# The last MLP's second pair of down chunks: eight of 16 k tiles in seven products instead of four, in three of its four quarters

## The chip, the cores and the metric

The kernel runs on one core of a Trainium2 chip. Its engines work side by side, each through its own instructions in order: PE (matrix multiply; the profile lists its weight loads apart as PEld), DVE (vector), ACT (scalar), POOL, and SP, which only issues transfers here. The metric is the device time of one execution in microseconds (us). A matrix product writes to PSUM; all other operands lie in SBUF, and weights come from HBM by DMA.

## The reference

A trunk of two layers on 256 tokens of width 2048. Each layer has a token mixer, an attention to a memory of 256 rows and an MLP with hidden width 8192; at the end stands a final norm. All in float32. The change touches the MLP of the second layer only:

```python
def squared_relu_mlp(h, w_up, w_down):
    return jnp.square(jax.nn.relu(h @ w_up)) @ w_down

for i in range(DEPTH):                      # 2 layers
    ...
    x = x + squared_relu_mlp(rms_norm(x, g_ff[i]), f_w_up[i], f_w_down[i])
return rms_norm(x, g_final)
```

## The kernel before

**Precision.** A float32 operand is split into a rounded high part and a remainder: ACT casts the high part (`whi`, `hh`), DVE subtracts to get the low part (`wlo`, `hl`), both in `split` (lines 103 and 104). A product is three matmuls, high by high, low by high and high by low. Every weight chunk of 128 x 1024 that is multiplied therefore costs ACT one cast and DVE one subtraction, whatever PE does with it.

**Tiling of the MLP.** `mlp` goes through the hidden width in four quarters `b`. Each quarter has an up part, which makes 2048 hidden features (four pairs of `hh` and `hl` tiles, eight calls of `gemm_feat`, four weight chunks each), and a down part, which multiplies these 16 k tiles by the quarter's rows of `w_down` and adds the result to `x`. The down part has four chunks `n` of 512 output columns. In the last MLP (`nxt.closing`) they go in two pairs, (0, 1) and (2, 3), through `gemm_seven`; only in the last quarter the chunks 2 and 3 go by plain products.

**Seven products.** For two halves of the tokens, two chunks of columns and two halves of some k tiles, a product has eight blocks of six matmuls. `gemm_seven` makes it of seven blocks, with sums of the hidden values (`token_sums`, made once per quarter) and four sums of weights. Named by the halves (k half, column chunk) of the weights, these sums are T1 = raw(0,1) - raw(0,0), T2 = raw(1,1) - T1, T3 = raw(1,1) - raw(0,1) and T4 = raw(1,0) - T2; each is one DVE subtraction of 128 x 1024, and each is then split like a chunk. The first four k tiles go this way in every pair (tiles `ws` and `run`; four of their split results go to a pair of buffers of their own, `own`). With `ahead`, four further k tiles go the same way (tile `more`: four raw chunks, and two slots for sums). What is left goes in plain products, `direct`, one weight chunk for two blocks. So a pair with `ahead` has 14 blocks of seven products and 8 plain chunks, a pair without has 7 and 12. Before the change, the first pair of every quarter has `ahead`, and the second has not.

**What sets the order.** A scheduler orders each engine's instructions by their priority and by what is free, when the kernel is built; on the chip each engine keeps that order. SP's queue issues all weight loads in one order, and a load whose buffer is still read holds back all behind it. Buffers: four for `wraw` (plain chunks), four for `ws`, three for the split pair `whi`/`wlo`, two for `own`, one tile `more` at a time. `block_ahead` (line 726) loads the four raw chunks of `more` and returns a function that makes its first three sums (lines 733 to 735); the fourth is made in `gemm_seven` (line 827). `gather` (line 687) adds a finished block to `x`; `keep` (line 800) has ACT copy an intermediate sum from PSUM to `more`.

Of the kernel before, what the change touches and what calls it, by code (L numbers as in the profile page):

```python
# [13 lines left out]
ALU = mybir.AluOpType  # L14
# [3 lines left out]
D = 2048  # L18
S = 256
KT = D // P  # L20
NB = 512
NCH = D // NB
KB = 2
# [6 lines left out]
DFF = 4 * D  # L30
# [8 lines left out]
class Trunk:  # L39
# [604 lines left out]
    def mlp(self, x, layer, cur, nxt):  # L644
        nc, a, tc = self.nc, self.a, self.tc
        wu, wd = a["f_w_up"][layer], a["f_w_down"][layer]
        hT = cur.act
        with tc.tile_pool(name="ml", bufs=4, reuse_waits="tile") as mp:
            r2 = mp.tile([P, 32 if layer else 24], F32, name="r2", bufs=1)[:, 0:2]
            ws = lambda: mp.tile([P, KB * NB], F32, name="ws", bufs=4)  # L650
            run = lambda: mp.tile([P, KB * NB], F32, name="run", bufs=1)
            kept = lambda i: more[:, 6 + i // 2, i % 2 * NB:i % 2 * NB + NB]
            self.fifth = None if nxt.closing else mp
            for b in range(DFF // D):
                hid = []
                for n in range(NCH):
                    h = mp.tile([P, 4, S], F32R, name="hh")
                    l = mp.tile([P, 4, S], F32R, name="hl")
                    rs = []
                    for i in range(2):  # L660
                        r = mp.tile([P, 2, S], F32, name="r", bufs=2)
                        self.gemm_feat(hT, wu, 2 * (NCH * b + n) + i, r)
                        nc.vector.scalar_tensor_tensor(out=r, in0=r, scalar=0.0, in1=r, op0=ALU.max, op1=ALU.mult)
                        self.split(h[:, 2 * i:2 * i + 2], l[:, 2 * i:2 * i + 2], r)
                        rs.append(r)
                    hid.append((h, l))
                    if nxt.closing and n == 0:
                        sums = []
                    if nxt.closing and n < 2:
                        sums.append(self.token_sums(ws(), lambda: mp.tile([P, 4, 2, P], F32R, name="sums", bufs=4), *rs))  # L670
                    if nxt.closing and n == NCH - 2:
                        more = self.act.tile([P, 8, KB * NB], F32, name="more", tag="act")
                        ahead = self.block_ahead(more, wd, b * KT)
                if nxt.closing:
                    ahead[-1]()
                if nxt.closing:
                    own = lambda: mp.tile([P, KB * NB], F32R, name="own", bufs=2)
                    nxt.room = lambda: mp.tile([P, 2, NB], F32, name="g", tag="ws", bufs=4)
                if b == 0:
                    rstd = cur.rstd()  # L680
                    nc.vector.tensor_tensor(out=r2, in0=rstd, in1=rstd, op=ALU.mult)
                if b == DFF // D - 1 and not nxt.closing:
                    nxt.start()

                def gather(t, n, part, cs=None):
                    xc = x[:, t, cs or slice(n * NB, (n + 1) * NB)]
                    nc.vector.scalar_tensor_tensor(out=xc, in0=part, scalar=r2[:, t:t + 1], in1=xc,
                                                   op0=ALU.mult, op1=ALU.add)

                for n in range(NCH):  # L690
                    end = b == DFF // D - 1
                    if nxt.closing and not (end and n >= NCH - 2):
                        if n % 2 == 0:
                            self.gemm_seven((ws, run, kept), lambda kt, t: [f[:, kt % 4, t * P:(t + 1) * P]
                                                                            for f in hid[kt // 4]],
                                            sums, wd, n, b * KT, gather, own=own, ahead=ahead if n == 0 else None)
                            if end:
                                nxt.start()
                    elif nxt.closing and end and n == NCH - 1:
                        self.gemm_last(hid, wd, n, b * KT, lambda t, acc: nxt.finish(x, t, lambda cs: gather(  # L700
                            t, n, acc[:, cs.start - n * NB:cs.stop - n * NB], cs)))
                        break
                    else:
                        acc = self.gemm_hid(hid, wd, n, b * KT)
                        for t in range(2):
                            gather(t, n, acc[:, t, :])
                    if end:
                        self.at(4 + n if nxt.closing and n < 2 else 1, lambda n=n: nxt.chunk(x, n))

            self.fifth = None  # L710
# [12 lines left out]
        self.split(sh, sl, s)  # L723
        return sh, sl

    def block_ahead(self, tile, w, k0):
        v = self.nc.vector
        raw = {(i, j): tile[:, 2 * i + j] for i in range(2) for j in range(2)}
        for (i, j), t in raw.items():
            self.fed = self.nc.sync.dma_start(out=t.rearrange("p (k c) -> p k c", k=KB), in_=w[j, k0 // KB + 2 + i]).ins  # L730

        def add():
            v.tensor_tensor(out=tile[:, 4], in0=raw[0, 1], in1=raw[0, 0], op=ALU.subtract)
            v.tensor_tensor(out=tile[:, 5], in0=raw[1, 1], in1=tile[:, 4], op=ALU.subtract)
            v.tensor_tensor(out=raw[0, 1], in0=raw[1, 1], in1=raw[0, 1], op=ALU.subtract)
        return raw, tile[:, 4], tile[:, 5], add

    def gemm_seven(self, tiles, token, sums, w, n0, k0, gather, end=None, own=None, ahead=None):

# [3 lines left out]
        v = nc.vector  # L745
        kc0 = k0 // KB
        ws, run, kept = tiles
        raw, half = {}, lambda t: t.rearrange("p (k c) -> p k c", k=KB)
# [45 lines left out]
        def whole(*a):  # L794
            for _ in direct(*a):
                pass
# [16 lines left out]
        block((0, 0), 0, 1, raw[1, 0], far.get((1, 0)))  # L813
        whole(1, 1)
        v.tensor_tensor(out=run, in0=raw[1, 1], in1=run, op=ALU.subtract)
        summed((1, 0), 1, run, t2)
        gather(0, n0, m1)
        u2 = keep((1, 0), 2)
        whole(1, 1)
        v.tensor_tensor(out=raw[0, 1], in0=raw[1, 1], in1=raw[0, 1], op=ALU.subtract)  # L820
        summed((1, 0), 2, raw[0, 1], far.get((0, 1)))
        gather(0, n0 + 1, u2)
        u3 = keep((1, 0), 3)
# [4 lines left out]
        block((1, 0), 1, 1, run, t1)  # L828
        whole(1, 1)
        summed((0, 1), 3, raw[1, 1], far.get((1, 1)))  # L830
        v.tensor_tensor(out=u3, in0=u3, in1=m5, op=ALU.add)
        whole(0, 0)
        gather(1, n0 + 1, u3)
        while len(todo[0]) > 1 or len(todo[1]) > 1:
            j = len(todo[1]) > len(todo[0])
            whole(j, j)
        ends = [direct(0, 1), direct(1, 0)]
        for keys in (((1, 0), (0, 1)), ((0, 0), (1, 1))):
            for e in ends:
# [774 lines left out]
```

## Time and profile before

| what | value |
|---|---|
| median of 3 runs | 2776.56 us (2775.83 to 2779.21) |
| the profiled execution | 2781.7 us, its span 2780.0 us, granted TensorE clock 0.998 |
| PE busy in the span | 2755.7 us (99%), 14996 matmuls |
| DVE, ACT busy | 2025.2 us (73%), 1410.3 us (51%) |
| DMA | 593.74 MB, 214 GB/s on average |
| last MLP's quarter 0: up part | from about 2076 to 2167.4 us |
| its first pair, second pair | 2167.4 to 2208.5, 2208.5 to 2250.9 us |
| quarters 1, 2 and 3: first pair starts at | 2340.0, 2512.5 and 2685.0 us |

Times in rows of the profile are from the start of the span. The duration of a matmul in a row includes its way through the array; matmuls overlap, so that the distance between two starts, and not the duration, is what one costs.

### The profile page before, as it was taken

Reading aid. Unit: us, or ns where it says so; the run is one execution under the profiler, and the core shown is the slowest. Engines: PE = TensorE matmul, PEld = TensorE weight load, DVE = VectorE, ACT = ScalarE, POOL = GpSimd, SP = SyncE. Lnnn points to the kernel's source line nnn. Section 1 sums busy time; section 2 is a strip of 40 time slices with the busy share of each in tenths; the row PEclk is TensorE's granted clock in tenths of the full one; section 3 lists DMA queues with packets and bytes.
Section 4 is the critical chain, followed back from the end, with each engine's and each line's share of the span. In section 5 each row is a group of like instructions: output and inputs, shape, how many; then the busy total and the mean of one; then the engine's idle time right before and its main releaser. Section 6 shows DMA issues by size and latency. Waiting matters only on the chain. (4 is left out here: it accounts for less than half of the span.)

```text
span 2780.0 us, 39477 instructions
## 1 busy us (share of the span) xinstructions
PE 2755.7 (99%) x14996; PEld 2330.6 (84%) x14996; DVE 2025.2 (73%) x2788; ACT 1410.3 (51%) x1805; POOL 187.0 (7%) x331
## 2 busy tenths in 40 slices
PE   9999999999999999999999999999999999999998
PEld 7888888888888888888887888888888888888887
DVE  6765756778888878787567657557777868778685
ACT  6445544555534444444556445445555545446454
POOL 0100000001011111120212100000000000000000
PEclk9999999999999999999999999999999999999999
DMA  8766665547788888886879766565557466564655
GB/s 295 225 201 232 200 182 181 169 159 237 216 278 260 261 257 259 265 259 214 237 246 272 221 200 228 176 194 154 182 175 226 148 215 199 194 220 148 217 182 158
DMA packets 194174, 593.74 MB, mean 214 GB/s; under 512 B 44096, under 2 KB 45168, under 8 KB 193472
## 3 DMA queue, kind: packets, MB, share of 16 engines
q1 hardware_dynamic: 153456, 537.46, 61.2%
q0 software_dynamic: 40000, 52.71, 6.8%
q8 instruction: 117, 1.92, 0.3%
q10 hardware_dynamic: 528, 1.06, 0.1%
q14 instruction: 73, 0.60, 0.1%
HBM read 567.51 MB, written 23.46 MB: 213 GB/s over the span
## 5 line engine op out<-in xcount | busy, mean ns | idle before, releaser
L104 DVE TENSOR_TENSOR wlo<-wraw,whi 128x1024 fp32r<-128x1024 f32 (+1 forms) x877 | 1065.1, 1221 | 442.2 <-ACT whi L103 435.9
L103 ACT CAST whi<-wraw 128x1024 fp32r<-128x1024 f32 (+1 forms) x877 | 920.6, 1051 | 833.2 <-PE acc L764 180.3
L174 PE MATMUL acc<-act,whi 128*128 128x512 f32 x3072 | 742.0, 392 | 3.3 <-ACT whi L103 2.2
L174 PEld LDWEIGHTS acc<-act,whi 128*128 128x128 f32 x3072 | 563.2, 188 | 114.0 <-ACT whi L103 2.6
L179 PEld LDWEIGHTS acc<-act,wlo 128*128 128x128 f32 x3072 | 396.3, 192 | 17.8 <-DVE wlo L104 2.1
L179 PE MATMUL acc<-act,wlo 128*128 128x256 f32 x3072 | 404.6, 284 | 1.5 <-DVE wlo L104 1.0
L159 PE MATMUL acc<-whi,act 128*128 128x512 f32 x1472 | 369.5, 393 | 5.6 <-ACT whi L103 5.6
L159 PEld LDWEIGHTS acc<-whi,act 128*128 128x128 f32 x1472 | 274.8, 189 | 62.8 <-ACT whi L103 5.8
L764 PE MATMUL acc<-whi,act 128*128 128x512 f32 x864 | 232.9, 392 | 0.1
L855 PE MATMUL acc<-whi,hl 128*128 128x512 f32 x544 | 212.7, 391 | 0.0
L854 PE MATMUL acc<-whi,hh 128*128 128x512 f32 x544 | 212.6, 391 | 0.0
L159 PE MATMUL acc<-wlo,act 128*128 128x512 f32 x736 | 197.6, 390 | 0.2 <-DVE wlo L104 0.2
L764 PEld LDWEIGHTS acc<-whi,act 128*128 128x128 f32 x864 | 160.4, 188 | 36.7 <-ACT ends L800 1.9
L159 PEld LDWEIGHTS acc<-wlo,act 128*128 128x128 f32 x736 | 138.3, 188 | 29.8 <-DVE wlo L104 1.0
L857 PE MATMUL acc<-wlo,hh 128*128 128x512 f32 x544 | 145.8, 389 | 0.0
L764 PE MATMUL acc<-wlo,act 128*128 128x512 f32 x432 | 133.1, 390 | 0.0
L764 PE MATMUL acc<-whi,hh 128*128 128x512 f32 x338 | 132.7, 393 | 0.0
L764 PE MATMUL acc<-whi,hl 128*128 128x512 f32 x338 | 131.6, 389 | 0.0
L190 ACT COPY r<-acc 128x512 f32<-128x512 f32 x64 | 37.7, 589 | 165.9 <-PE acc L174 165.8
L855 PEld LDWEIGHTS acc<-whi,hl 128*128 128x128 f32 x544 | 102.1, 188 | 22.2 <-issue 1.0
L854 PEld LDWEIGHTS acc<-whi,hh 128*128 128x128 f32 x544 | 102.1, 188 | 21.4 <-issue 0.2
L857 PEld LDWEIGHTS acc<-wlo,hh 128*128 128x128 f32 x544 | 102.1, 188 | 21.4 <-issue 0.2
(375 smaller groups left out, 2813.3 us busy)
## 6 DMA issues: line engine op xcount, KB each, us to landing
wraw<-in_f_w_up SPq DMA_DIRECT2D x256, 512.0 KB, 4.6
wraw<-in_f_w_down SPq DMA_DIRECT2D x212, 512.0 KB, 5.1
wraw<-in_x_w_q SPq DMA_DIRECT2D x64, 512.0 KB, 4.2
wraw<-in_x_w_k SPq DMA_DIRECT2D x64, 512.0 KB, 4.2
wraw<-in_b_w_out SPq DMA_DIRECT2D x64, 512.0 KB, 4.4
wraw<-in_a_w_in SPq DMA_DIRECT2D x63, 512.0 KB, 4.7
wraw<-in_x_w_v SPq DMA_DIRECT2D x48, 512.0 KB, 4.3
wraw<-in_x_w_o SPq DMA_DIRECT2D x48, 512.0 KB, 4.2
```

The source lines that it names most:

```text
L103: self.nc.scalar.copy(out=hi, in_=src)
L104: return self.nc.vector.tensor_tensor(out=lo, in0=src, in1=hi.bitcast(F32), op=ALU.subtract).ins
L159: nc.tensor.matmul(out[t], a[:, kt, sl], b[:, kk, :], start=st and a is ah, stop=en)
L174: nc.tensor.matmul(acc[:, f, :], hi[:, kk, sl], both[:, kt].rearrange("p a s -> p (a s)"), start=first and kk == 0, stop=last and kk == FK ...
L179: nc.tensor.matmul(acc[:, f, 0:S], lo[:, kk, sl], ah[:, kt, :], start=False, stop=last and kk == FK - 1, skip_group_check=True)
L190: nc.scalar.copy(out=dst, in_=acc[:, :, S:])
L764: mm = lambda s, m, e: nc.tensor.matmul(out, s, m, start=key not in begun, stop=e, skip_group_check=True)
L854: nc.tensor.matmul(acc[:, t, :], ah, hi[:, kk, :], start=kt == 0, stop=False)
L855: nc.tensor.matmul(acc[:, t, :], al, hi[:, kk, :], start=False, stop=False)
L857: nc.tensor.matmul(acc[:, t, :], hid[kt // 4][0][:, kt % 4, sl], lo[:, kk, :], start=False, stop=kt == KT - 1)
```

## The change

The second pair of the quarters 0, 1 and 2 gets `ahead` as well. `mlp` now makes one object by `block_ahead` for each pair that has it (two in quarters 0 to 2, one in quarter 3); both use the same tile `more` of the quarter. `block_ahead` no longer loads at once: it returns a function that loads and one that makes chosen sums. The first pair's loads are issued in the up part, now tied in SP's order behind the last weight load, and its three sums are tied on DVE behind the last split. The second pair's loads are issued from inside the first pair, as the raw chunks in `more` come free; its first sum stands near the end of the first pair, its second and third inside the second pair, each next to the corresponding sum of the first four k tiles. The two slots for sums change roles between the pairs (`turn`).

```diff
@@ mlp @@
-                        ahead = self.block_ahead(more, wd, b * KT)
+                        ahead = [self.block_ahead(more, wd, 2 * j, b * KT, j) for j in range(1 if b == DFF // D - 1 else 2)]
+                        ahead[0][-2]()
                 if nxt.closing:
-                    ahead[-1]()
+                    ahead[0][-1](0, 1, 2)
...
-                                            sums, wd, n, b * KT, gather, own=own, ahead=ahead if n == 0 else None)
+                                            sums, wd, n, b * KT, gather, own=own, ahead=ahead[n // 2],
+                                            then=ahead[1] if n == 0 and len(ahead) > 1 else None)
@@ block_ahead @@
-    def block_ahead(self, tile, w, k0):
+    def block_ahead(self, tile, w, n0, k0, turn=0):
         v = self.nc.vector
         raw = {(i, j): tile[:, 2 * i + j] for i in range(2) for j in range(2)}
-        for (i, j), t in raw.items():
-            self.fed = self.nc.sync.dma_start(out=t.rearrange("p (k c) -> p k c", k=KB), in_=w[j, k0 // KB + 2 + i]).ins
-
-        def add():
-            v.tensor_tensor(out=tile[:, 4], in0=raw[0, 1], in1=raw[0, 0], op=ALU.subtract)
-            v.tensor_tensor(out=tile[:, 5], in0=raw[1, 1], in1=tile[:, 4], op=ALU.subtract)
-            v.tensor_tensor(out=raw[0, 1], in0=raw[1, 1], in1=raw[0, 1], op=ALU.subtract)
-        return raw, tile[:, 4], tile[:, 5], add
+        t1, t2 = (tile[:, 4 + (k + turn) % 2] for k in range(2))
+
+        def load():
+            for (i, j), t in raw.items():
+                src = w[n0 + j, k0 // KB + 2 + i]
+                with self.tc.issue_after(self.fed):
+                    self.fed = self.nc.sync.dma_start(out=t.rearrange("p (k c) -> p k c", k=KB), in_=src).ins
+
+        made = set()
+
+        def add(*ks):
+            for k in ks:
+                if k not in made:
+                    out, p, q = ((t1, raw[0, 1], raw[0, 0]), (t2, raw[1, 1], t1), (raw[0, 1], raw[1, 1], raw[0, 1]))[k]
+                    with self.tc.issue_after(self.low):
+                        v.tensor_tensor(out=out, in0=p, in1=q, op=ALU.subtract)
+                    made.add(k)
+        return raw, t1, t2, load, add
@@ gemm_seven @@
         v.tensor_tensor(out=run, in0=raw[1, 1], in1=run, op=ALU.subtract)
+        if ahead:
+            ahead[-1](1)
         summed((1, 0), 1, run, t2)
...
         v.tensor_tensor(out=raw[0, 1], in0=raw[1, 1], in1=raw[0, 1], op=ALU.subtract)
+        if ahead:
+            ahead[-1](2)
...
         summed((0, 1), 3, raw[1, 1], far.get((1, 1)))
+        if then:
+            then[-2]()
...
             whole(j, j)
+        if then:
+            then[-1](0)
```

Three places show how the change moves instructions. In the rows, a name left of the arrow is written and the names right of it are read; line numbers above 700 differ between the two kernels.

**DVE, start of the second pair of quarter 0.** Before: the four gathers of the first pair (`x<-acc`), then splits of the first four k tiles and of plain chunks.

```order
L687 SCALAR_TENSOR_TENSOR x<-acc,r_18745,x 128x512 x2
L104 TENSOR_TENSOR wlo<-ws,whi 128x1024
L687 SCALAR_TENSOR_TENSOR x<-acc,r_18745,x 128x512 x2
L104 TENSOR_TENSOR wlo<-wraw,whi 128x1024
L104 TENSOR_TENSOR own<-run,own 128x1024
L104 TENSOR_TENSOR wlo<-wraw,whi 128x1024
L687 SCALAR_TENSOR_TENSOR x<-more,r_18745,x 128x512
L104 TENSOR_TENSOR wlo<-wraw,whi 128x1024
L825 TENSOR_TENSOR run<-ws,run 128x1024
L104 TENSOR_TENSOR own<-ws,own 128x1024
```

Now:

```order
L688 SCALAR_TENSOR_TENSOR x<-acc,r_18745,x 128x512 x2
L104 TENSOR_TENSOR wlo<-more,whi 128x1024
L104 TENSOR_TENSOR own<-run,own 128x1024
L104 TENSOR_TENSOR wlo<-ws,whi 128x1024
L104 TENSOR_TENSOR wlo<-more,whi 128x1024
L104 TENSOR_TENSOR wlo<-wraw,whi 128x1024
L746 TENSOR_TENSOR more<-more 128x1024
L688 SCALAR_TENSOR_TENSOR x<-more,r_18745,x 128x512
L841 TENSOR_TENSOR run<-ws,run 128x1024
L104 TENSOR_TENSOR wlo<-more,whi 128x1024
L104 TENSOR_TENSOR wlo<-wraw,whi 128x1024
L746 TENSOR_TENSOR more<-more 128x1024
```

Splits of `more` have come between those of `ws` and `wraw`, and two sums of `more` stand behind splits of plain chunks; the sum behind the next plain chunk (line 843) follows a few rows later.

**DVE, end of the up part of quarter 0**, around the last two results of the up part (`r<-acc`). Before:

```order
L191 TENSOR_TENSOR r<-acc,r 128x512
L663 SCALAR_TENSOR_TENSOR r<-r 128x512
L104 TENSOR_TENSOR wlo<-wraw,whi 128x1024 x2
L104 TENSOR_TENSOR hl<-r,hh 128x512
L104 TENSOR_TENSOR wlo<-more,whi 128x1024
L827 TENSOR_TENSOR more<-more 128x1024
L104 TENSOR_TENSOR wlo<-ws,whi 128x1024
L191 TENSOR_TENSOR r<-acc,r 128x512
```

Now:

```order
L104 TENSOR_TENSOR hl<-r,hh 128x512
L746 TENSOR_TENSOR more<-more 128x1024
L834 TENSOR_TENSOR ws<-ws 128x1024
L746 TENSOR_TENSOR more<-more 128x1024 x2
L104 TENSOR_TENSOR wlo<-more,whi 128x1024
L104 TENSOR_TENSOR wlo<-ws,whi 128x1024
L191 TENSOR_TENSOR r<-acc,r 128x512
```

Four sums now stand in a row ahead of the first split of `more`. Before, the three of them on `more` were made earlier: in quarter 0 at the start of the MLP, in the later quarters near the end of the down part before. The fourth sum of `more` (line 827 before, 843 now) has moved back into the pair.

**SP, loads during the down part of quarter 0.** Before (the `more` chunks are those of quarter 1's first pair):

```order
L752 DMA ws<-in_f_w_down 128x1024
L127 DMA wraw<-in_f_w_down 128x1024 x9
L730 DMA more<-in_f_w_down 128x1024
L127 DMA wraw<-in_f_w_down 128x1024 x2
L730 DMA more<-in_f_w_down 128x1024
L127 DMA wraw<-in_f_w_down 128x1024
L730 DMA more<-in_f_w_down 128x1024 x2
```

Now (the single `more` loads are those of quarter 0's second pair, those of quarter 1 come later):

```order
L764 DMA ws<-in_f_w_down 128x1024
L737 DMA more<-in_f_w_down 128x1024
L127 DMA wraw<-in_f_w_down 128x1024 x2
L737 DMA more<-in_f_w_down 128x1024
L764 DMA ws<-in_f_w_down 128x1024 x2
L737 DMA more<-in_f_w_down 128x1024
L127 DMA wraw<-in_f_w_down 128x1024
L764 DMA ws<-in_f_w_down 128x1024
L127 DMA wraw<-in_f_w_down 128x1024
L737 DMA more<-in_f_w_down 128x1024
L127 DMA wraw<-in_f_w_down 128x1024 x8
L127 DMA wraw<-in_f_w_up 128x1024 x22
```

The loads of `more` have moved forward into the first pair, between those of `ws`. Behind the 22 up chunks follow a load of `ws`, two more up chunks and then all four loads of `more` for the next first pair; two of the remaining `ws` loads now stand behind the 30th up chunk and the last behind the 32nd.

More of the change, by code (lines that the diff above doesn't have):

```diff
@@ L724, in token_sums, with gemm_seven @@
         return sh, sl
-    def block_ahead(self, tile, w, k0):
+    def block_ahead(self, tile, w, n0, k0, turn=0):
         v = self.nc.vector
         raw = {(i, j): tile[:, 2 * i + j] for i in range(2) for j in range(2)}
-        for (i, j), t in raw.items():
-            self.fed = self.nc.sync.dma_start(out=t.rearrange("p (k c) -> p k c", k=KB), in_=w[j, k0 // KB + 2 + i]).ins
-        def add():
-            v.tensor_tensor(out=tile[:, 4], in0=raw[0, 1], in1=raw[0, 0], op=ALU.subtract)
-            v.tensor_tensor(out=tile[:, 5], in0=raw[1, 1], in1=tile[:, 4], op=ALU.subtract)
-            v.tensor_tensor(out=raw[0, 1], in0=raw[1, 1], in1=raw[0, 1], op=ALU.subtract)
-        return raw, tile[:, 4], tile[:, 5], add
-    def gemm_seven(self, tiles, token, sums, w, n0, k0, gather, end=None, own=None, ahead=None):
+        t1, t2 = (tile[:, 4 + (k + turn) % 2] for k in range(2))
[13 more added lines that the diff above has]
+        return raw, t1, t2, load, add
+    def gemm_seven(self, tiles, token, sums, w, n0, k0, gather, end=None, own=None, ahead=None, then=None):
         nc = self.nc
```

## The prediction

> **What bounds the kernel now.** I read the page's engine shares first, then busy time by stretch in quarter 0's down part, then the timeline of PE at the edges of its pairs.
>
> ```profile
> PE 2755.7 (99%) x14996; PEld 2330.6 (84%) x14996; DVE 2025.2 (73%) x2788; ACT 1410.3 (51%) x1805; POOL 187.0 (7%) x331
> 2166.50:2208.80 42.30, 42.30 (x187) 34.53 (x186) 36.19 (x36) 26.14 (x29) 0.00 (x0) 1.00 0.46 150
> 2208.80:2251.00 42.20, 42.20 (x187) 34.63 (x186) 31.12 (x31) 20.54 (x23) 0.00 (x0) 1.00 0.64 211
> ```
>
> The columns of the stretches are length, then busy time and count of PE, PEld, DVE, ACT, POOL, then granted clock, DMA share and GB/s. PE is busy throughout both pairs at full clock; DVE is busy 86% of the first and 74% of the second. So PE bounds this part, and a matmul less is time less, as long as DVE, which feeds it, stays ahead.
>
> ```profile
> 2167.42 1.52 PE L764 MATMUL acc<-own,sums 128*128 128x512 f32 x6
> 2208.54 1.52 PE L764 MATMUL acc<-own,sums 128*128 128x512 f32 x6
> 2250.90 1.98 PE L174 MATMUL acc<-act,whi 128*128 128x512 f32 x8
> ...
> 2512.54 1.52 PE L764 MATMUL acc<-own,sums 128*128 128x512 f32 x6
> 2553.60 1.52 PE L764 MATMUL acc<-own,sums 128*128 128x512 f32 x6
> 2595.97 1.98 PE L174 MATMUL acc<-act,whi 128*128 128x512 f32 x8
> ```
>
> These are the first matmuls of the first pair, of the second and of the next up part, in quarters 0 and 2. First pairs take 41.12 and 41.06 us, second pairs 42.36 and 42.37. The first pair is already what the second is to become, so the profile holds a precedent. It also waits little:
>
> ```profile
> PEld acc L764 <- ACT more L800: 0.9, 4, 0.2
> PEld acc L764 <- DVE wlo L104: 0.2, 1, 0.2
> ```
>
> That is all of PE's waiting in quarter 0's down part (total, times, longest): four short waits for an intermediate sum to be copied out, and one for a split.
>
> **PE's saving.** By the code a first pair has 14 blocks of six matmuls and 8 plain chunks of twelve, 84 + 96 = 180; a second pair 7 and 12, 42 + 144 = 186. One matmul costs the distance of two starts:
>
> ```profile
> 2215.34 1.52 PE L764 MATMUL acc<-own,sums 128*128 128x512 f32 x6
> 2216.70 0.39 PE L764 MATMUL acc<-whi,hh 128*128 128x512 f32 x1
> ```
>
> Six take 1.36 us, one 0.227. Three pairs lose 18 matmuls: 18 x 0.227 = 4.1 us. Between the measured pairs the difference is 1.24 and 1.31 us, three times the mean 3.8; I take 3.8, since it holds the waits that this form of pair brings.
>
> The Trainium skill, "TensorE: Matmul & The Clock Gate", section "Back-to-back issue gap", puts a sustained stream of weight loads and matmuls at about 131 ns per matmul of 512 columns; the saving would then be estimated at 18 x 0.131 = 2.4 us. The row disagrees: this stream of just such pairs costs 227 ns, so the measurement decides.
>
> **What DVE and ACT take on.** A second pair splits 22 chunks in place of 19 and makes four more sums, while three sums for the next quarter leave its tail: net three casts on ACT and four operations on DVE. Per operation:
>
> ```profile
> L103 ACT CAST whi<-more x28: 1048/1056/1061, 2162.1 to 2708.2; 128x1024 fp32r<-128x1024 f32 x28
> L104 DVE TENSOR_TENSOR wlo<-more,whi x28: 1214/1218/1226, 2163.2 to 2709.3; 128x1024 fp32r<-128x1024 f32 x28
> L733 DVE TENSOR_TENSOR more<-more x4: 1225/1226/1226, 2086.5 to 2578.5; 128x1024 f32<-128x1024 f32 x4
> 2171.31 1.22 DVE L104 TENSOR_TENSOR own<-run,own 128x1024 fp32r<-128x1024 f32 x1
> 2172.45 1.22 DVE L104 TENSOR_TENSOR wlo<-ws,whi 128x1024 fp32r<-128x1024 f32 x1
> 2173.58 1.22 DVE L104 TENSOR_TENSOR wlo<-more,whi 128x1024 fp32r<-128x1024 f32 x1
> ```
>
> In a row, DVE starts one every 1.14 us. So DVE's second pair grows by about 4 x 1.14 = 4.5 us to 35.7 of some 41.1 us, 87%, the share at which the first pair runs; ACT by 3.2 to 23.7. On average nothing is exposed; what counts is the dense first half. There DVE begins where the gathers end:
>
> ```profile
> 2209.15 1.40 DVE L687 SCALAR_TENSOR_TENSOR x<-acc,r,x 128x512 f32<-128x512 f32 x2
> 2210.47 1.22 DVE L104 TENSOR_TENSOR wlo<-wraw,whi 128x1024 fp32r<-128x1024 f32 x1
> 2218.67 0.75 DVE L687 SCALAR_TENSOR_TENSOR x<-more,r,x 128x512 f32<-128x512 f32 x1
> 2219.34 1.22 DVE L104 TENSOR_TENSOR wlo<-run,whi 128x1024 fp32r<-128x1024 f32 x1
> ...
> 2186.40 1.06 ACT L103 CAST whi<-more 128x1024 fp32r<-128x1024 f32 x1 [0.30 <-PE acc L764]
> ```
>
> From 2210.47 on the new order has 18 operations of 1.14 and two gathers (0.67 to the next start) up to the split of the plain chunk that PE uses from its 19th group of six: 21.9 us, to 2232.4. PE begins that group at 2208.54 + 18 x 1.36 = 2233.0 and needs the low part four matmuls later, 2233.9: DVE is 1.5 us ahead. The tighter points are those where the split pair's three buffers decide: a buffer comes free two groups (2.72 us) before its next use, the low part is needed 0.91 later, and the cast (which follows PE by 0.30 in the last row) and the split take 0.3 + 1.06 + 1.22 = 2.6: 1.0 us ahead. That holds in the first pair too. Each new sum stands just behind the split of a plain chunk, which occupies PE for 2.72 us and DVE for 1.14, so none stands between a buffer coming free and its split. I cost them at nothing. Without that cover a sum costs PE 1.14 us; the other end, a gain, has no source here.
>
> **The start of the MLP.** In quarter 0 the old sums stand among the norm's work:
>
> ```profile
> 2086.53 1.23 DVE L733 TENSOR_TENSOR more<-more 128x1024 f32<-128x1024 f32 x1 [1.21 <-DMA more<-in_f_w_down]
> 2087.67 0.87 DVE L246 SCALAR_TENSOR_TENSOR act<-ps,gcol,act 128x256 fp32r<-128x256 f32 x2
> 2086.73 0.50 PE L179 MATMUL acc<-act,wlo 128*128 128x256 f32 x2 [0.34 <-ACT act L245]
> 2088.21 3.25 PE L174 MATMUL acc<-act,whi 128*128 128x512 f32 x13 [0.51 <-DVE act L246]
> ```
>
> DVE waits 1.21 us for a load, then makes a sum, and the norm's operation behind it is what PE waits 0.51 us for. The sum leaves. Bounds: 0, since a split now stands between the two norm operations, and 0.34 + 0.51 = 0.85. I take -0.4, nearest the one wait that names L246.
>
> **The end of the up part.** Four quarters get four sums in a row (4 x 1.14 = 4.5 us) ahead of the first split of `more`:
>
> ```profile
> 2160.71 0.68 DVE L104 TENSOR_TENSOR hl<-r,hh 128x512 fp32r<-128x512 f32 x1
> 2163.19 1.23 DVE L104 TENSOR_TENSOR wlo<-more,whi 128x1024 fp32r<-128x1024 f32 x1 [1.79 <-ACT whi L103]
> 2168.24 0.69 DVE L191 TENSOR_TENSOR r<-acc,r 128x512 f32<-128x512 f32 x1 [1.43 <-ACT r L190]
> 2169.68 0.61 PE L764 MATMUL acc<-wlo,sums 128*128 128x512 f32 x2
> ```
>
> The split ends at 2164.4 and PE needs it at 2169.7: 5.3 us ahead. With the four sums from 2161.3 it starts at 2165.9 and ends at 2167.1, 2.6 ahead; the rest of the rows fits before the `r<-acc` at 2168.24, which waits for PE as before. In return the fourth `more` sum leaves and the tight split (the 0.2 wait) comes earlier. Queued behind the sums are those splits and the last two `r<-acc`, and PE waits for the splits first. New on SP: two `ws` loads behind the 30th up chunk, one behind the 32nd.
>
> ```profile
> 2150.39 0.68 DVE L104 TENSOR_TENSOR hl<-r,hh 128x512 fp32r<-128x512 f32 x1
> 2137.42 13.41 SPq L127 DMA_DIRECT2D wraw<-in_f_w_up  x6
> DMA to landing us min/median/max: 3.7/4.5/6.9
> ```
>
> The last six up loads go out at 2137.4 to 2150.8; a `ws` load after the last lands near 2155.4 (4.5), at worst 2157.8 (6.9, the landing times of `ws`). In the new order a sum and three splits stand between the `hl` that ends at 2151.1 and the sum that reads this chunk, so DVE reaches it at 2151.1 + 4 x 1.14 = 2155.7: 0 to 2.1 us late, inside the 2.6. Bounds per quarter: -0.2 (the wait that goes) to +0.2 (one such wait more). I take +0.1, over four quarters about +0.3.
>
> **Other loads.** The bytes stay the same. Four `more` loads leave the tail of the second pair and four for the second pair go between the `ws` loads of the first, where DMA share is 0.46. Each waits for a split of the chunk it replaces; the last of those is of group 22 of 30, near 2167.4 + 21 x 1.36 = 2196, landing by 2203, and the sum that reads it stands five operations behind 2210.47, near 2216. Nothing.
>
> **Sum.** -3.8 - 0.4 + 0.3 = -3.9 us. The profiled execution, 2781.7 with its span of 2780.0, would become 2777.8; it lies 5.1 above the median, so I carry the difference over: 2776.56 - 3.9 = 2772.7 us. About 0.2% (5.55 us) is what a measurement here can tell from no change, and this is 0.14%.
>
> **Rivals.** *The gain is whole and the waits go too.* 4.1 for the matmuls, 0.85 at the start, 0.2 in three quarters: -5.6, 2771.0. For it: both waits have named causes that move. Against: new pairs bring copy waits. Chance 0.12.
>
> *Late sums eat the gain.* In each changed pair one sum is exposed, because its load or an ACT cast is late: 3 x 1.14 = 3.4, leaving -0.5: 2776.1. For it: 1.0 us ahead is less than one sum. Against: the dense first pair shows one wait of 0.2. Chance 0.13.
>
> *DVE paces the second pair.* If its lead is lost at the start, all four sums of a pair lie on PE's path, since nothing gives the lead back in the dense half: 3 x 4 x 1.14 = 13.7, less 3.8 and 0.4: +9.5, 2786.1, slower. It decides from 1.0 us of lateness at the first split of `more`, for example by a load held back on SP. For it: 87% busy, no slack in 22 us. Against: plain chunks give 1.6 us each. Chance 0.08.
>
> That the pairs don't save is excluded: the new order has 18 matmuls less.
>
> By the Trainium skill, "VectorE: DVE Perf Modes", section "The DRAIN you can't avoid", the next operation does not start until the one before has emptied; the lead after 18 operations would then be 1.5 - 18 x 0.08, about nothing, with the same sum. The starts above, 1.14 apart at a duration of 1.22, disagree.
>
> **How the numbers follow.** The forecast holds 0.67, with its own range 2771.3 to 2774.5. Faster by over 0.2% is below 2771.0: half of the first rival, 0.06, and 0.10 for a median that falls low, as the three runs span 3.4 us: 0.16. Slower is the third rival, 0.08. Within 0.2%: 0.76. The range 2770.4 to 2777.6 takes in the first two rivals and leaves out the third and the tails.
>
> **What would show it.** Second pairs of 41.0 to 41.4 us in three quarters, first pairs and quarter 3 as before; PE's waits there still 0.2 each; L246's wait at the start below 0.51; the first split of `more` ending before PE's low matmuls. Wrong would be second pairs above 42.4, DVE waits for `ws` or `more` loads over 2 us at the up part's end, or PE waits for `wlo` of about 1.1.

## The result, and the profile after

The changed kernel takes 2771.22 us (median of 21 runs, 2767.81 to 2776.06), the kernel before 2777.02 us beside it (21 runs, 2774.05 to 2782.98): a ratio of 0.9979, interval 0.9973 to 0.9986. That is 5.8 us or 0.21% faster, at the edge of what a measurement of this kernel can tell. The forecast was 3.9 us. The time lies in the predicted range, 0.1 below the forecast's own range (2771.3 to 2774.5) and on the value of the rival "the gain is whole and the waits go too" (2771.0).

The profiled execution took 2768.95 us, its span 2767.2. That is 12.8 us below the profiled execution of before, and about half of it is not the change: the first matmul of the last MLP already starts 6.8 us earlier (2068.37 against 2075.15), in work that the change does not touch. So I compare stretches inside the last MLP, from one start of a matmul to another. First the edges of the pairs in the timeline of PE, kernel after, quarters 0 and 2 (start, duration, what):

```profile
2068.37 1.98 PE L174 MATMUL acc<-act,whi 128*128 128x512 f32 x8
2159.84 1.52 PE L776 MATMUL acc<-own,sums 128*128 128x512 f32 x6
2200.85 1.52 PE L776 MATMUL acc<-own,sums 128*128 128x512 f32 x6
2241.65 1.52 PE L174 MATMUL acc<-act,whi 128*128 128x512 f32 x6
...
2501.60 1.52 PE L776 MATMUL acc<-own,sums 128*128 128x512 f32 x6
2542.62 1.52 PE L776 MATMUL acc<-own,sums 128*128 128x512 f32 x6
2583.42 0.84 PE L174 MATMUL acc<-act,whi 128*128 128x512 f32 x3
```

A second pair now takes 40.80 us (2241.65 - 2200.85), a first pair 41.01. The same differences for all quarters, in us, from the timelines of both kernels:

| stretch | before | after | difference |
|---|---|---|---|
| first up matmul to the first pair of quarter 0 | 92.27 | 91.47 | -0.80 |
| first pairs, quarters 0, 1, 2 | 41.12, 41.13, 41.06 | 41.01, 41.01, 41.02 | -0.27 |
| second pairs, quarters 0, 1, 2 | 42.36, 42.37, 42.37 | 40.80, 40.80, 40.80 | -4.70 |
| up parts of quarters 1, 2, 3 | 89.07 each | 89.07 each | 0 |
| first pair of quarter 3 to the last matmul | 84.40 | 84.30 | -0.10 |
| sum | 694.29 | 688.42 | -5.87 |

The sum agrees with the difference of the medians, 5.8. The page's engine shares, kernel after:

```profile
PE 2747.1 (99%) x14978; PEld 2326.5 (84%) x14978; DVE 2046.0 (74%) x2809; ACT 1421.1 (51%) x1814; POOL 186.7 (7%) x331
```

The busy time by stretch of quarter 0's two pairs (columns as in the prediction):

```profile
2159.84:2200.85 41.01, 41.01 (x181) 33.63 (x180) 38.70 (x39) 25.87 (x29) 0.00 (x0) 1.00 0.64 205
2200.85:2241.65 40.80, 40.80 (x181) 33.78 (x180) 34.23 (x34) 23.80 (x26) 0.00 (x0) 1.00 0.40 116
```

There are 18 matmuls less. The second pair is 180 x 0.2267 = 40.81 us of matmuls and nothing else: PE does not wait in it at all. What PE waits for in both pairs of quarter 0, from the waits of after (total, times, longest), and then the two rows of weight loads in its timeline:

```profile
PEld acc L776 <- ACT more L812: 0.5, 2, 0.2
```

```profile
2174.77 0.19 PEld L776 LDWEIGHTS acc<-whi,hh 128*128 128x128 f32 x1 [0.23 <-ACT more L812]
2180.32 0.19 PEld L776 LDWEIGHTS acc<-whi,hh 128*128 128x128 f32 x1 [0.24 <-ACT more L812]
```

Before there were four waits for a copy, two in each pair, and one for a split. The waits of before in its second pair (2208.5 to 2250.9):

```profile
PEld acc L764 <- ACT more L800: 0.5, 2, 0.2
```

The two of the second pair and the one for a split have gone. The two that are left belong to the first pair, and they are all that separates 41.01 from 40.80: a wait listed with 0.23 us costs PE 0.1.

**Why the copies of the second pair are now in time** stands in the timeline of ACT, kernel after; first a copy of the first pair, then one of the second (the bracket is idle time ahead and what ended it):

```profile
2171.83 1.06 ACT L103 CAST own<-ws 128x1024 fp32r<-128x1024 f32 x1 [0.30 <-PE acc L776]
2173.19 1.06 ACT L103 CAST whi<-wraw 128x1024 fp32r<-128x1024 f32 x1 [0.30 <-PE acc L776]
2174.15 0.57 ACT L812 COPY more<-acc 128x512 f32<-128x512 f32 x1
...
2212.84 1.06 ACT L103 CAST own<-ws 128x1024 fp32r<-128x1024 f32 x1 [1.04 <-PE acc L776]
2214.65 0.59 ACT L812 COPY more<-acc 128x512 f32<-128x512 f32 x1 [0.76 <-PE acc L776]
```

In the first pair a cast stands between PE's result and its copy, and the copy starts when the cast is through. In the second pair ACT has nothing to do ahead of the copy and stands ready.

**The end of the up part.** The timeline of DVE, kernel after, quarter 0, and the matmuls that need the first split of `more`:

```profile
2143.17 1.23 DVE L821 TENSOR_TENSOR run<-ws 128x1024 f32<-128x1024 f32 x1 [0.48 <-DMA ws<-in_f_w_down]
2148.92 1.23 DVE L827 TENSOR_TENSOR run<-ws,run 128x1024 f32<-128x1024 f32 x1 [0.95 <-DMA ws<-in_f_w_down]
2156.41 2.35 DVE L746 TENSOR_TENSOR more<-more 128x1024 f32<-128x1024 f32 x2
2158.68 1.22 DVE L104 TENSOR_TENSOR wlo<-more,whi 128x1024 fp32r<-128x1024 f32 x1
2162.11 0.62 PE L776 MATMUL acc<-wlo,sums 128*128 128x512 f32 x2
```

DVE does wait for the `ws` loads that went back behind up chunks, 0.48 and 0.95 us, and the split of `more` still ends at 2159.90, 2.2 us ahead of PE. The forecast was 2.6.

**The second pair's lead**, same view, with the matmuls that need these splits:

```profile
2205.06 1.22 DVE L104 TENSOR_TENSOR wlo<-ws,whi 128x1024 fp32r<-128x1024 f32 x1
2207.20 0.61 PE L776 MATMUL acc<-wlo,hh 128*128 128x512 f32 x2
2211.40 1.22 DVE L104 TENSOR_TENSOR wlo<-more,whi 128x1024 fp32r<-128x1024 f32 x1
2214.00 0.61 PE L776 MATMUL acc<-wlo,sums 128*128 128x512 f32 x2
2222.28 1.22 DVE L104 TENSOR_TENSOR wlo<-more,whi 128x1024 fp32r<-128x1024 f32 x1
2224.88 0.61 PE L776 MATMUL acc<-wlo,hh 128*128 128x512 f32 x2
2223.49 1.23 DVE L104 TENSOR_TENSOR wlo<-wraw,whi 128x1024 fp32r<-128x1024 f32 x1
2226.24 0.61 PE L776 MATMUL acc<-wlo,hh 128*128 128x512 f32 x2
```

DVE is only 0.9 us ahead at a split of `ws` near the start of the pair (2207.20 - 2206.28), before any of the pair's own sums of `more`. Behind these sums it is 1.4 us ahead at the split of the second sum (2214.00 - 2212.62), 1.4 at a later split of `more` (2224.88 - 2223.50) and 1.5 at the plain chunk of the 19th group (2226.24 - 2224.72), as forecast for that one.

### The profile page after: what moved, and what is told of

Read it like the earlier page. It is cut to its first block, busy times and chain, and to the rows that moved or that the text cites. A ratio compares the mean times of both kernels' runs of the same rounds, so it can differ in the third digit from the quotient of the medians.

```text
span 2767.2 us, 39486 instructions
## 1 busy us (share of the span) xinstructions
PE 2747.1 (99%) x14978; PEld 2326.5 (84%) x14978; DVE 2046.0 (74%) x2809; ACT 1421.1 (51%) x1814; POOL 186.7 (7%) x331
## 3 DMA queue, kind: packets, MB, share of 16 engines
q10 hardware_dynamic: 528, 1.06, 0.1%
## 5 line engine op out<-in xcount | busy, mean ns | idle before, releaser
L104 DVE TENSOR_TENSOR wlo<-wraw,whi 128x1024 fp32r<-128x1024 f32 (+1 forms) x865 | 1051.3, 1221 | 444.5 <-ACT whi L103 438.2
L103 ACT CAST whi<-wraw 128x1024 fp32r<-128x1024 f32 (+1 forms) x865 | 909.2, 1053 | 812.2 <-PE acc L875 181.2
L776 PE MATMUL acc<-whi,act 128*128 128x512 f32 x864 | 233.0, 392 | 0.1
L875 PE MATMUL acc<-whi,hl 128*128 128x512 f32 x544 | 212.7, 391 | 0.0
L874 PE MATMUL acc<-whi,hh 128*128 128x512 f32 x544 | 212.6, 391 | 0.0
L776 PEld LDWEIGHTS acc<-whi,act 128*128 128x128 f32 x864 | 160.3, 188 | 36.8 <-ACT ends L812 1.9
L776 PE MATMUL acc<-wlo,act 128*128 128x512 f32 x432 | 133.1, 390 | 0.0
L190 ACT COPY r<-acc 128x512 f32<-128x512 f32 x64 | 37.7, 589 | 162.9 <-PE acc L174 162.8
L776 PE MATMUL acc<-whi,hh 128*128 128x512 f32 x308 | 120.5, 391 | 0.0
L776 PE MATMUL acc<-whi,hl 128*128 128x512 f32 x308 | 119.9, 389 | 0.0
```

The costliest lines, as they stand in the source:

```text
L103: self.nc.scalar.copy(out=hi, in_=src)
L104: return self.nc.vector.tensor_tensor(out=lo, in0=src, in1=hi.bitcast(F32), op=ALU.subtract).ins
L190: nc.scalar.copy(out=dst, in_=acc[:, :, S:])
L776: mm = lambda s, m, e: nc.tensor.matmul(out, s, m, start=key not in begun, stop=e, skip_group_check=True)
L874: nc.tensor.matmul(acc[:, t, :], ah, hi[:, kk, :], start=kt == 0, stop=False)
L875: nc.tensor.matmul(acc[:, t, :], al, hi[:, kk, :], start=False, stop=False)
```

## The experiments

Two questions stay open after the traces. The first is how the gain divides into fewer matmuls, order of loads and sums, and waits that go. The second is whether the third rival (DVE paces the second pair) was far or near. In each run I give the median where there are several executions, and the stretches of its profile, which repeat to 0.04 us between kernels that do the same there.

**1. The saving alone.** The kernel before, with one block of six matmuls left out of each second pair; that part of the sum is missing from the output.

```diff
             for t in (first, 1 - first):
-                into((t, j), range(KB), lambda kk: token(KB * kc + kk, t), hi, lo)
+                if not (own and not ahead and kc == 6 and j == 0 and t == 1):
+                    into((t, j), range(KB), lambda kk: token(KB * kc + kk, t), hi, lo)
```

> The kernel before, with one block of six matmuls (one plain chunk, one token half) left out of each second pair of quarters 0 to 2, so its output lacks that part of the sum. Nothing else moves: DVE, ACT and SP have the rows of before. Theory A, the gain of the change is three separate parts (18 matmuls 4.1 us, the waits inside the second pairs 0.6, the start of the MLP and one wait per first pair 1.1): 4.1 us less than before, second pairs of 41.0 us (42.36 - 1.36), not 40.8, since the two short waits for copies stay. Rival B, the matmuls count less because the time of a pair is set by DVE and ACT, and the gain of the change comes from where its sums and loads stand: second pairs above 41.5 us, less than 2.5 us gained.

Measured: 2772.71 us (2770.96 to 2780.45, 10 runs), 0.9986 of before (0.9977 to 0.9995). The second pairs take 41.00, 41.00 and 41.01 us, 1.36 less than before. In its second pair (waits from 2195 to 2250) the two waits for a copy are still there:

```profile
PEld acc L764 <- ACT more L801: 0.5, 2, 0.2
```

So the matmuls are worth 3 x 1.36 = 4.08 us, and with the same number of matmuls the changed kernel is another 0.20 a pair faster, which is these two waits.

**2. The order alone.** The changed kernel with its held-back loads and sums, but without `ahead` in the second pairs.

```diff
-                        ahead = [self.block_ahead(more, wd, 2 * j, b * KT, j) for j in range(1 if b == DFF // D - 1 else 2)]
+                        ahead = [self.block_ahead(more, wd, 2 * j, b * KT, j) for j in range(1)]
...
-                                            sums, wd, n, b * KT, gather, own=own, ahead=ahead[n // 2],
+                                            sums, wd, n, b * KT, gather, own=own, ahead=ahead[0] if n == 0 else None,
```

> The change without its seven products: the first pair's loads and its three sums are held back as in the change, the second pair stays with 7 and 12 blocks, 186 matmuls. Theory A: 1.1 us less than before, 0.8 of it ahead of the first pair of quarter 0 (the two waits in the norm shrink to one of 0.34) and 0.1 in each first pair (the wait for a split goes); second pairs stay at 42.4 us. Rival B: 3 us or more gained. Rival C, holding sums back costs, since four stand in a row: first pairs above 41.3 us.

Measured: 2775.90 us (2771.91 to 2780.17, 10 runs), 0.9994 (0.9985 to 1.0003), which the times alone can't tell from no change. Its profile can: from the first up matmul to the last matmul 693.16 us, 1.13 less than before. Of these 0.80 lie at the start, 0.24 in the three first pairs (41.01, 41.02, 41.04) and 0.08 in quarter 3. The second pairs are those of before, 42.37, 42.37 and 42.36, with their two waits for a copy. With the first run this divides the whole: 4.08 matmuls, 0.6 waits in the second pairs, 1.1 order.

**3. The sums early again.** The changed kernel, but the first pair's loads and sums are no longer tied behind the last load and the last split of the up part; only the second pair's are.

```diff
-                with self.tc.issue_after(self.fed):
+                with self.tc.issue_after(self.fed) if turn else nullcontext():
...
-                    with self.tc.issue_after(self.low):
+                    with self.tc.issue_after(self.low) if turn else nullcontext():
```

> The change with the first pair's loads and sums free to stand early, as in the kernel before; the second pair takes eight k tiles in seven products and makes its sums as in the change. Theory A: 4.7 us less than before (18 matmuls and the pairs' waits), the start of the MLP as before with 0.51 and 0.34 us of waits, first pairs as before at 41.1; second pairs 40.8 to 41.0 although DVE then makes three more sums in each (about 37.7 us busy of 40.8). Rival D, DVE paces the pair once it is over 90% busy: second pairs above 41.5 us and less than 2.6 us gained.

Measured: 2771.47 us (2767.19 to 2774.10, 7 runs), 0.9977 (0.9966 to 0.9987). First pairs are back at 41.09, 41.12 and 41.12 with the wait for a split (`PEld acc L776 <- DVE wlo L104`, 0.2), second pairs stay at 40.80, with DVE busy for 35.38 us of them (37.7 were expected). The start takes 91.98 us. So the tie is what moves the first pairs by 0.1 and the start; the second pairs owe it nothing. From the first up matmul to the last matmul it takes 4.99 us less than before; the 0.29 beyond the expected 4.7 are all at the start.

The start is worth a look of its own, since before and runs 1 and 3 all make the first sum there and yet lose different amounts. The timelines of DVE, first run 1, then run 3; before stands in the prediction (1.21):

```profile
2081.37 1.23 DVE L733 TENSOR_TENSOR more<-more 128x1024 f32<-128x1024 f32 x1 [0.60 <-DMA more<-in_f_w_down]
```

```profile
2077.30 1.23 DVE L746 TENSOR_TENSOR more<-more 128x1024 f32<-128x1024 f32 x1 [0.92 <-DMA more<-in_f_w_down]
```

DVE waits 0.60, 0.92 and 1.21 us for the load, and the stretch takes 91.66, 91.98 and 92.27: step for step the same. Without the sum it takes 91.47 (changed kernel and run 2). So the first 0.4 us of the wait are hidden, and all beyond lies on PE's path. What the change saves there is the wait for one load less 0.4, and that differs between executions: 0.2 to 0.8 in these three.

**4. The first pair's sums spread too.** The changed kernel, but only the first of the three sums of the first pair is made in the up part; the others go to the places inside the pair.

```diff
-                    ahead[0][-1](0, 1, 2)
+                    ahead[0][-1](0)
```

> The change, with two of the first pair's three sums of the added k tiles moved into the pair as well, to the places they have in a second pair. Against the change: theory A', the two 0.1 us copy waits of a first pair come from ACT making a cast ahead of the copy, and go where the order on ACT becomes that of a second pair: first pairs of 40.8 us in place of 41.0, 0.8 us less in four quarters, so 6.6 less than before. Rival D: with 38.5 us of DVE work and 2.3 more in 40.8, DVE paces the first pair: 41.5 us or more, 2 us lost against the change.

Measured: 2771.73 us (2768.35 to 2774.10, 11 runs), 0.9981 (0.9973 to 0.9990), not to be told from the changed kernel. First pairs take 40.88, 40.89 and 40.89, 0.13 less. The expected 40.80 was missed because the waits for a copy go but one for a split comes back (listed 0.2, cost 0.08). Rival D falls: DVE is busy for 39.51 of these 40.88 us. ACT at the first pair's first waiting copy, timeline of this kernel:

```profile
2175.09 1.06 ACT L103 CAST own<-ws 128x1024 fp32r<-128x1024 f32 x1 [0.30 <-PE acc L776]
2176.90 0.59 ACT L812 COPY more<-acc 128x512 f32<-128x512 f32 x1 [0.76 <-PE acc L776]
```

Here too the wait vanishes exactly where no cast stands in front of the copy. First pair or second makes no difference.

**5 to 7. How near DVE was.** In the second pairs sums of `more` are made again, with the same values, so DVE carries one, two or three subtractions more. The edit of run 5 (run 6 adds the line twice; run 7 adds it once, and makes the third sum, into the slot of the first, and the fourth sum once more each):

```diff
                     with self.tc.issue_after(self.low):
                         v.tensor_tensor(out=out, in0=p, in1=q, op=ALU.subtract)
+                        if turn and k == 1:
+                            v.tensor_tensor(out=out, in0=p, in1=q, op=ALU.subtract)
```

> The kernel with the change, but in the three second pairs the second sum of `more` is made twice (the same values again), so that DVE carries one subtraction of 1.14 us more there. Nothing is left out. In the order as built, two operations then stand ahead of the split of that sum that stood behind it in the change, and PE has moved two matmuls (0.45 us) ahead of the ones that need it. Theory L (what matters is DVE's lead at single splits; the profile of the change gives 1.4 us at this one, 2214.00 against 2211.40 + 1.22): 2 x 1.14 - 1.4 - 0.45 = 0.4 us of wait in each second pair, so 41.2 us where the change has 40.80, and 1.3 us over the three; at most 0.9 a pair if the moved matmuls give nothing. Rival B (what matters is the share of DVE in a pair, 84% now): the sum fits into the 16% that are idle, second pairs stay at 40.80.

> As the run before, with that sum made three times in all: two subtractions, 2.3 us, more on DVE in each second pair (about 90% of 40.8, less than the 94% of the first pair). Nothing is left out. Theory L: three operations ahead of the split, 3 x 1.14 - 1.4 - 0.45 = 1.6 us a pair (up to 2.0), second pairs at 42.4 to 42.8 and 4.8 to 6 us over the three, that is, the whole gain of the change is gone although DVE is busy for less of the pair than in the first one. Rival B: 40.80, since 16% of 40.8 is 6.5 us and only 2.3 are taken.

> The third rival of the prediction (DVE paces the second pair) made on purpose: in each second pair the second sum three times, and the third and fourth sums twice, four subtractions more in all, 4.6 us, so that DVE is asked for about 38.8 of 40.8 us, 95%. Nothing is left out. Theory L: once the lead of 1.4 us is used up, each further sum lies on PE's path at 1.14 us: about 4 x 1.14 - 1.4 - 0.2 = 3.0 us a pair, second pairs at 43.8 and 9 us over the three, a time near 2780, slower than before by 3. Rival B: at 95% the sums still fit, second pairs at 40.80 to 41.1, as the first pair, which runs at 94%.

The last expectation speaks of four subtractions more. The edit of run 7 makes three: its second pair has 37 operations on DVE, the changed kernel's 34 (counts in the rows below and above). The 3.0 us expected there rest on a wrong count.

Measured, in us. The third column tells how many operations more than in the changed kernel stand ahead of the split that is late; the text behind the rows says which it is:

| run | subtractions more per second pair | operations more ahead of the late split | second pairs | more than 40.80 | expected |
|---|---|---|---|---|---|
| 5 | 1 | 2 | 41.66, 41.67, 41.71 | 0.88 | 0.4 to 0.9 |
| 6 | 2 | 3 | 42.95, 42.93, 42.94 | 2.14 | 1.6 to 2.0 |
| 7 | 3 | 4 | 43.86, 43.86, 43.85 | 3.06 | 3.0, for four subtractions |

All other stretches are those of the changed kernel. The times: 2770.70 us and 2774.77 us, one execution each, and for run 7 2779.07 us (2775.86 to 2783.54, 8 runs), 1.0010 of before (0.9998 to 1.0021). Rival B, which goes by DVE's share, falls in all three. Busy time of run 6's second pair, then run 7's two pairs:

```profile
2200.26:2243.21 42.95, 41.27 (x181) 33.50 (x180) 36.53 (x36) 23.60 (x26) 0.00 (x0) 1.00 0.36 111
```

```profile
2160.75:2201.78 41.03, 41.03 (x182) 33.63 (x181) 38.97 (x39) 25.88 (x29) 0.00 (x0) 1.00 0.63 205
2201.78:2245.64 43.86, 41.83 (x182) 33.40 (x181) 37.64 (x37) 23.55 (x26) 0.00 (x0) 1.00 0.35 107
```

DVE does less in these slow second pairs (36.53 and 37.64 us) than in the first pair of 41.03 (38.97). PE's waits in runs 5 and 6, rows of weight loads:

```profile
2214.06 0.30 PEld L778 LDWEIGHTS acc<-wlo,sums 128*128 128x128 f32 x2 [0.29 <-DVE wlo L104]
2215.20 0.30 PEld L778 LDWEIGHTS acc<-wlo,hh 128*128 128x128 f32 x2 [0.84 <-DVE wlo L104]
```

```profile
2214.34 0.76 PEld L778 LDWEIGHTS acc<-whi,sums 128*128 128x128 f32 x4 [2.10 <-ACT whi L103]
2215.30 0.19 PEld L778 LDWEIGHTS acc<-whi,hh 128*128 128x128 f32 x1 [0.19 <-ACT whi L103]
2216.74 0.30 PEld L778 LDWEIGHTS acc<-wlo,hh 128*128 128x128 f32 x2 [0.23 <-DVE wlo L104]
```

In runs 5 and 6 the late split is that of the second sum, and besides the added subtractions the fourth sum has moved ahead of it. With two operations ahead the price is 2 x 1.14 - 1.4 = 0.88, as measured. The matmuls that the order moves forward (four in run 5, where two were expected) give nothing: the next split, of a plain chunk, is late as well. With three ahead the sum is so late that its cast is late as well, and the wait moves from `wlo` to `whi`: 2.14, a little above 3 x 1.14 - 1.4 = 2.0. Two more subtractions undo the whole gain of a second pair (1.57).

In run 7 the split of the second sum has one operation more ahead of it, and PE loses 0.1 there. The late split is that of the third sum. First it and the matmuls that need it in the changed kernel, then the split in run 7 and PE's two longest waits there:

```profile
2216.61 1.22 DVE L104 TENSOR_TENSOR wlo<-more,whi 128x1024 fp32r<-128x1024 f32 x1
2219.44 0.61 PE L776 MATMUL acc<-wlo,sums 128*128 128x512 f32 x2
```

```profile
2222.22 1.22 DVE L104 TENSOR_TENSOR wlo<-more,whi 128x1024 fp32r<-128x1024 f32 x1
2221.34 0.76 PEld L780 LDWEIGHTS acc<-whi,sums 128*128 128x128 f32 x4 [2.05 <-ACT whi L103]
2224.62 0.30 PEld L780 LDWEIGHTS acc<-wlo,hh 128*128 128x128 f32 x2 [0.84 <-DVE wlo L104]
```

Counted from the start of the pair, the split starts at 15.76 us in the changed kernel and at 20.45 in run 7. That is 4.7 us or four operations later: two added sums, and a fourth sum and a split of `own` that the new order put ahead. Its lead was 1.6 us (2219.44 - 2217.83), so 3.1 us should lie on PE's path, and 3.06 do. Theory L holds, but by the operations ahead of a split and not by the added ones; the 3.0 of the expectation was met by luck.

**8. The copy ahead of the cast.** The changed kernel, but in all pairs of the last MLP the cast of a plain chunk stands behind the second and third copy.

```diff
-            nc.scalar.copy(out=t, in_=banks[key])
+            copied.append(nc.scalar.copy(out=t, in_=banks[key]).ins)
...
-            hi, lo = self.wtile(w, n0 + j, kc0 + kc)
+            with self.tc.issue_after(copied[-1]) if own and len(copied) > 2 else nullcontext():
+                hi, lo = self.wtile(w, n0 + j, kc0 + kc)
```

> The kernel with the change, but in all pairs of the last MLP the cast of the next plain chunk is tied behind the second and third copy of an intermediate sum on ACT, so that no cast of a plain chunk stands just ahead of such a copy. Nothing is left out. Theory C (PE's waits for the copies come from ACT's order: a cast of 1.06 us starts 0.4 us before the copy could): the copy waits of the first pairs go, 40.8 to 40.9 us where the change has 41.01, about 0.2 us a pair, and second pairs stay at 40.80; over the whole kernel some -0.7 us, below what the times can tell, so the profile decides. Rival D (a copy that hands a bank back to PE costs PE 0.1 us by itself): first pairs stay at 41.0, with the two waits for a copy. If the later casts come too late, PE waits for `whi` or `wlo` instead, and first or second pairs grow.

Measured: 2794.93 us (2794.51 to 2799.54, 3 runs), 1.0072 (1.0047 to 1.0097): clearly slower. The waits for a copy are gone from both pairs, as Theory C has it, but every pair takes 44.6 us where 40.8 to 40.9 were expected: the casts now come too late. ACT and PE in the first pair, timeline of this kernel:

```profile
2173.66 0.59 ACT L813 COPY more<-acc 128x512 f32<-128x512 f32 x1 [0.76 <-PE acc L776]
2174.14 1.05 ACT L103 CAST whi<-wraw 128x1024 fp32r<-128x1024 f32 x1
2173.01 0.61 PE L776 MATMUL acc<-wlo,sums 128*128 128x512 f32 x2
2175.24 0.50 PE L776 MATMUL acc<-whi,hh 128*128 128x512 f32 x1 [1.62 <-ACT whi L103]
```

The two matmuls at 2173.01 would have been followed at 2173.46; PE goes on at 2175.24, when the cast that now starts at 2174.14 is through. That is 1.8 us, 1.9 with the slower start of the matmuls behind it, and a second time in each pair (44.63 - 40.80 = 3.83 for both), for 0.1 saved twice in a first pair. The cast was not in the copy's way by chance: it is what PE needs first, and the short wait is the cheap end of a bad choice.

## Why the prediction was right, and where it was off

**What bounds the part** was right: PE at full clock, a matmul less is time less. All of the gain lies where the edits are, and nothing elsewhere paid for it.

**The saving** was mis-sized. 18 x 0.227 = 4.1 stands: run 1 measures 3 x 1.36 = 4.08. The step that failed is the next: "I take 3.8, since it holds the waits that this form of pair brings". The second pairs gained 4.70, and at 40.80 us they lie below the 41.0 to 41.4 that were to show it. The first pairs' waits were a property of ACT's order at two copies and not of the form, and the second pair in its old form already had such waits to lose, which were counted in its 42.37. The profile of before said so: two of its four waits for a copy lie in the second pair. I took a difference of two neighbours for a precedent without asking what the neighbours wait for. On the price of one matmul, the Trainium skill, "TensorE: Matmul & The Clock Gate", section "Back-to-back issue gap", with its 131 ns would give an estimate of 0.8 us for the six of run 1; the run gives 1.36.

**DVE and ACT** at nothing was right, and by the reason given: the lead was computed as 1.5 us at the 19th group and is 1.5. DVE's load was put too high, at 35.7 us; it is 34.23, since the first of the pair's four sums is made in the first pair. The starts 1.14 apart carry the lead. By the rule weighed there (the Trainium skill, "VectorE: DVE Perf Modes", section "The DRAIN you can't avoid") it would have been about nothing. The same section adds that a next operation that is not held starts earlier, which the prediction left out, and the rows agree with that: 1.14 us from start to start at a duration of 1.22. Of the leads shown above the smallest is 0.9, at the split of `ws`, close to the 1.0 that the prediction gave for splits that wait for a buffer. There it is DVE's own queue that makes the split late, as its cast (on ACT from 2203.32 for 1.06 us) is through 0.7 us before it starts. Behind the pair's sums the smallest is 1.4, at the split of the second sum, which the prediction did not single out.

**The start** was -0.4 and is -0.80, within the bounds 0 to -0.85. The step that failed is the choice "nearest the one wait that names L246": 0.51 was listed, 0.80 lost. A wait listed at a matmul is not its price, since ends of matmuls are modelled. The distance between starts is. Experiments 1 to 3 add that this term is the landing of one load and varies between executions.

**The end of the up part** was +0.3 and is about -0.1 in each quarter, -0.37 together. The late `ws` loads came as described, and the lead of 2.2 us took them. The wait for the tight split went, which was the lower bound; I took the upper side without a wait to point at.

**Other loads** at nothing was right: the up parts take 89.07 us before and after, and in quarter 0's two pairs DVE waits for no load.

**The rivals.** "The gain is whole and the waits go too" met the total, -5.6 against -5.87 in the profiles, in part by luck: its 0.2 in three quarters reads as the wait for a split, and that gave about 0.1 in each of four quarters, while the copy waits of the second pairs, 0.6 in all, were not in its sum. With 0.12 it was rated too low, as was faster by over 0.2% with 0.16. The argument against it, that new pairs bring waits for copies, rested on the precedent that failed. "Late sums eat the gain" did not occur. "DVE paces the second pair" did not occur either, but runs 5 to 7 show its mechanism. Its point of decision, put at 1.0 us of lateness at the first split of `more`, would by the rows be the 0.9 at the split of `ws`, as DVE goes from the split of `more` behind the gathers to that one without a gap; no run made that first split late. For the sums inside the pair it is 1.4. Its price of 1.14 us holds to 0.15 us per pair where the operations ahead of the late split are counted (2, 3 and 4), and with three subtractions more the kernel is no longer faster than before.

**What stays open**: what sets the landing of the first `more` load at the start, and whether quarter 3's second pair could go the same way, which was not tried.

## What to carry to other kernels

Whether added work on a feeding engine is free is read from its lead at each hand-over (when PE needs a tile, less when that tile is ready), not from its share of busy time: here 84% busy left room for 1.4 us behind the new sums and for 0.9 near the start of the pair, and the second added subtraction already cost more than a second pair had gained. Count the operations that stand ahead of the hand-over in the order as built: one added operation can bring another forward with it. When a neighbouring stretch serves as precedent, take its waits out first and ask of each what order causes it. Count the saved work at its measured pitch and price each wait by itself. A short wait may also be the cheap side of an order: look at what the blocking instruction feeds before moving it.

## What was not expected of the hardware

The idle time listed ahead of an instruction and the time lost differ in both directions: waits of weight loads listed with 0.23 us cost 0.10 (first pairs, 41.01 against 40.80), and a wait of a matmul listed with 0.51 went with a loss of 0.80 at the start of the MLP. The wait for one load, in three executions that have the same instructions around it, was 0.60, 0.92 and 1.21 us, and the time of the stretch followed it to 0.01 us.
